# Low parts of 42 weight units formed in an earlier stage and read back from DRAM; six expert blocks placed before the last loop

## The chip, the core and the metric

The kernel runs on one core of a Trainium2 chip. A core has four engines that compute: TensorE (PE, matrix products into PSUM), VectorE (DVE), ScalarE (ACT) and GpSimd (POOL), and SyncE (SP), which here issues DMAs. Each runs its own queue of instructions in order and waits on semaphores for the others. 16 DMA engines move data between DRAM and the on-chip SBUF. A DMA is issued by an engine's queue: SP's, ACT's and POOL's are used. The metric is the time of one execution on the device, in microseconds (us).

## The reference

Two transformer blocks over one sequence of 512 tokens of width 1024, all in float32. The first has four mixers (short convolution, sparse attention, latent attention, short convolution), each with a residual. The second has neighbourhood attention with a gated MLP beside it, then a PEER layer and a last norm; its vectors `c` and `c_ctx` are multiplied with `ada_w` into scales and shifts. The parts that the change touches are the second short convolution and the PEER layer:

```python
def short_conv_mixer(xn, w_in, conv_w, conv_b, w_out):
    bg, cg, hv, z = jnp.split(xn @ w_in, 4, axis=-1)
    u = cg * hv
    y = causal_depthwise_conv_of_width_3(u, conv_w) + conv_b
    return (bg * y * jax.nn.silu(z)) @ w_out

def block(xb):                                   # PEER, per block of tokens
    q = (xb @ wq).reshape(PEER_BLOCK, PEER_HEADS, 2, PEER_HALF)
    s = jnp.einsum('thpd,hpkd->thpk', q, sub_keys)
    s_top, i_top = lax.top_k(s, PEER_TOPK)
    ...                                          # all pairs of the two halves' best
    best_s, best_pos = lax.top_k(cand_s, PEER_TOPK)
    experts = jnp.take_along_axis(cand_i, best_pos, axis=-1)
    g = jax.nn.softmax(best_s, axis=-1)
    act = jax.nn.gelu(jnp.einsum('thkd,td->thk', expert_u[experts], xb))
    return jnp.einsum('thk,thkd->td', g * act, expert_v[experts])
```

There are 16384 experts (128 x 128), 8 heads and 16 experts per head and token.

## The kernel before

**Weights.** Each float32 product is made of three TensorE passes: a weight tile of 128 x 1024 (a unit, 0.5 MB) is split into a high part `whi`, a rounded copy made by ScalarE (line 69), and a low part `wlo`, the difference, made by VectorE (line 71). `gemm_t` (lines 254 to 262) multiplies high by high, high by low and low by high: 24 matmuls a unit. `Stream` feeds the units of all layers in one list: SP loads `wraw` up to four units ahead (line 57), the split runs up to two units ahead. `wraw` has two buffers (in the PEER layer every third unit has one from a further pool), `whi` and `wlo` four each.

**The second convolution** has 32 units of `a_in` and 8 of `a_out`, each against 512 tokens. After each of the first 32 the function `side(u)` is called for work that fills the other engines: it loads a tile of `ada_w` into `adaw` (two buffers, line 861) and VectorE reduces it (line 870).

**PEER layer.** First 16 projections (`p_wq`, 24 matmuls of 512 columns each), with the top 16 found by VectorE. The steps of `choose` then form the pairs and select the experts of one block of 128 tokens. The experts are computed densely for the first 320 tokens: `gates` scatters the chosen weights into a matrix of tokens by 16384 experts. It has 80 groups of 4 tokens. For each group `marks` builds two 0/1-like operands in `w` tiles, by VectorE (lines 1306 and 1307) or, for two groups in eight, by VectorE and ScalarE (lines 1298, 1301, 1302); four TensorE matmuls (line 1329) form the matrix, ScalarE copies it out (`stage`, line 1330), and after each eighth group a 2 MB store to `gsp` in DRAM goes through ScalarE's DMA queue (line 1336).

`s_part` (lines 1153 to 1163) is a block: the scores of 128 experts from one unit of `p_u`, 24 matmuls of 320 columns, then gelu on ScalarE (line 1160). The results of the first 12 blocks stay in SBUF. Those of the next 21 go into a tile `gr` (two buffers, which the loop's reads of `gsp` use as well) and are stored to `sgd` through ScalarE's queue (line 1162). Some blocks are set between the steps of `choose`, most among the gates (line 1333), and the rest after the last gate, before the loop.

**The loop** takes the 128 units of `p_v`, multiplies block results with `gsp`, read four units at a time into `gr`, and sums. Beside it GpSimd gathers the expert rows of the remaining tokens (line 1376) and VectorE multiplies them.

**What sets the order.** The order on each engine's queue is set when the program is built: a scheduler places the instructions of the loops above on each engine by its own estimate of when they can run. So a place in the source is not a place on a queue.

Of the kernel before, what the change touches and what calls it, by code (L numbers as in the profile page):

```python
# [10 lines left out]
F32 = mybir.dt.float32  # L11
F32R = mybir.dt.float32r
# [3 lines left out]
OP = mybir.AluOpType  # L16
# [3 lines left out]
D = 1024  # L20
KD = 8
# [4 lines left out]
AHEAD = 12  # L26
MORE = 21
EARLY = 2
LAG = 2
LOOK = 2  # L30
CLOCK = (1.0, 2.3, 1.0)
TD = 3
ND = 320
# [2 lines left out]
S_AT = (1, 4, 7)  # L36
# [3 lines left out]
class Stream:  # L40
# [3 lines left out]
    def __init__(self, nc, pools, units, ahead_load, ahead_split):  # L44
        self.nc, (self.raw, self.hi, self.lo) = nc, pools
        self.more = None
        self.units, self.pos, self.loaded, self.split = units, 0, 0, 0
        self.al, self.asp = ahead_load, ahead_split
        self.r, self.hl = {}, {}
# [13 lines left out]
    def _split(self, upto):  # L63
        nc = self.nc
        while self.split < min(self.loaded, upto):
            t = self.r.pop(self.split)
            n = t.shape[1]
            h = self.hi.tile([128, n], F32R, name="whi")
            nc.scalar.activation(h, t, AF.Copy)  # L69
            l = self.lo.tile([128, n], F32R, name="wlo")  # L70
            nc.vector.tensor_tensor(l, t, h.bitcast(F32), OP.subtract)  # L71
            self.hl[self.split] = (h, l)
            self.split += 1

# [8 lines left out]
def program(ctx, tc, A, out, upto=99, dbg=None):  # L83
    nc = tc.nc
# [20 lines left out]
    dram = ctx.enter_context(tc.tile_pool(name="dram", bufs=1, space=bass.MemoryType.DRAM))  # L105

    def big(shape, dt, name):
        return bigp.tile(shape, dt, name=name, tag="big")

    def bank(shape=(128, S), pool="a"):  # L110
        return psp[pool].tile(list(shape), F32, name="bank" + pool, tag="bank" + pool)
# [60 lines left out]
    W = Stream(nc, (wraw, whi, wlo), units, 4, 2)  # L172
# [99 lines left out]
    def split(src, h, l, scale=None):  # L272
        SC.activation(h, src, AF.Copy)  # L273
        V.tensor_tensor(l, src, h.bitcast(F32), OP.subtract)  # L274
# [854 lines left out]
    def peer(nrm, lp):  # L1129
# [14 lines left out]
        sg = {}  # L1144
# [83 lines left out]
        for m in range(16):  # L1228
# [10 lines left out]
            for t in range(NT):  # L1239
                v, n = val[:, t, m // 2, m % 2], ix[:, t, m // 2, m % 2]  # L1240
# [21 lines left out]
        def columns(g):  # L1262

            nf = tmp([128, 2, 128])
            ni = tmp([128, 2, 128], I32)
            V.tensor_scalar(ni[:, 0], ei, 7, 127, OP.logical_shift_right, OP.bitwise_and)
            V.tensor_scalar(ni[:, 1], ei, 127, None, OP.bitwise_and)
            V.tensor_copy(nf, ni)
            p = bank([128, 3, 128])
            for a, x in enumerate((nf[:, 1], g, nf[:, 0])):  # L1270
                PE.transpose(p[:, a], x, ident)
            T = hn.rearrange("p (a c x) -> p a c x", a=2, c=4)[:, next(turn)]
            SC.activation(T[:, :3], p, AF.Copy)
            SC.activation(T[:, 3], p[:, 1], AF.Copy, scale=-1.0)
            cols.append(T)
# [4 lines left out]
        def halves(g):  # L1280

            V.tensor_scalar(idx, ei, 16383, None, OP.bitwise_and)
            for dst, src in ((idx_h, idx), (gate_h, g)):
                V.tensor_copy(dst[HALF:], src[HALF:, HALF:])
                SC.dma_start(dst[:HALF], src[HALF:, :HALF])
# [3 lines left out]
        def marks(n):  # L1289


            T, t0 = cols[n // 32], n % 32 * 4
            oj, oi = tmp([128, 4, 128]), tmp([128, 4, 128])

            def each(c):
                return T[:, c, t0:t0 + 4, None].to_broadcast([128, 4, 128])
            if n % 8 in BY_ACT:
                V.tensor_tensor(oj, many, each(0), OP.is_equal)
                for a in range(4):
                    w, i, nw = (T[:, c, t0 + a:t0 + a + 1] for c in (1, 2, 3))  # L1300
                    SC.activation(oi[:, a], iota, AF.Abs, scale=-1.0, bias=i)
                    SC.activation(oi[:, a], oi[:, a], AF.Relu, scale=nw, bias=w)
            else:
                for a in range(4):
                    j, w = (T[:, c, t0 + a:t0 + a + 1] for c in range(2))
                    V.tensor_scalar(oj[:, a], iota, j, w, OP.is_equal, OP.mult)
                V.tensor_tensor(oi, many, each(2), OP.is_equal)
            return oj, oi

        def gates():  # L1310

            ready, steps = [], []
            for n in range(ND // 4):
                t, r = n // 32, n % 8
                if n % 32 == 0:
                    steps = []
                    if t < TD - 1:
                        g, steps = choose(t + 1)
                        steps.append(lambda g=g: columns(g))
                        if t == TD - 2:  # L1320
                            steps.append(lambda g=g: halves(g))
                if r == 0:
                    st = big([128, 128, 32], F32, "stage")
                while len(ready) + n < min(n + 1 + LOOK, ND // 4):
                    ready.append(marks(len(ready) + n))
                oj, oi = ready.pop(0)
                ps = bank([128, 4, 128])
                for a in range(4):
                    PE.matmul(ps[:, a], oj[:, a], oi[:, a], start=True, stop=True)
                SC.activation(st[:, :, r * 4:r * 4 + 4], ps.rearrange("p t i -> p i t"), AF.Copy)  # L1330
                if steps and r:
                    steps.pop(0)()
                if len(sg) < AHEAD + MORE - 3 and r in S_AT:
                    s_part()
                if r == 7:
                    SC.dma_start(gsp[:, :, n // 8].rearrange("c p x -> p c x"), st.rearrange("p (c i) t -> p c (i t)", i=4))
            assert not steps
# [15 lines left out]
        _, steps = choose(TD)  # L1353
# [93 lines left out]
        step, used, held, fetched = 0, 0, [], []  # L1447
        clock = np.cumsum([CLOCK[(i >= MORE) + (i >= 128 - AHEAD)] for i in range(128)])
        for i in range(128):
# [40 lines left out]
        for a in range(TD):  # L1490
            for x in held:
                value_part(a, *x)
            final(a)

    def conv_layer(j):

        def layer(nrm, after, lp, src, dst):
            def side(u):
                if u == 2:
                    ada_part.cb = conditions(2 - j)  # L1500
                elif u == 3 and j == 0:
                    angles()
                elif u >= 4 and 28 * j + u - 4 < min(28 + 28 * j, 48):
                    ada_part(lp, 28 * j + u - 4)
                if u == 32 and j:
                    hc.append(ctx_norm())
            short_conv(j, nrm, after, lp, src, dst, side)
        return layer
# [146 lines left out]
```

## Time and profile before

| what | us |
|---|---|
| runs | 2806.35, 2812.2, 2813.47 |
| median of the runs | 2812.2 |
| the profiled execution | 2807.74 |
| its span (first to last instruction) | 2805.9 |
| TensorE busy (matmul) | 2658.9 (95%) |
| TensorE busy (weight load, beside the matmuls) | 2299.7 (82%) |
| VectorE busy | 2222.7 (79%) |
| ScalarE busy | 1268.8 (45%) |
| GpSimd busy | 524.2 (19%) |
| DMA moved | 586.64 MB, 209 GB/s in the mean |

The span is what the trace covers; the profiled execution's own time is 1.8 us longer. Busy shares are means over stages of very different kinds, so the rows below go stage by stage: busy time by window, which wait ended idle time, single instructions in time, and DMAs from issue to landing. The chain of waits starts at the last instruction and follows back what released each step.

### The profile page before, as it was taken

The page shows a single profiled execution, that of the slowest core. Times are in us where ns is not written, and L with a number is a line of the kernel's source. Part 1 is how long each engine was busy: PE and PEld are TensorE (multiplying, and loading weights), DVE is VectorE, ACT ScalarE, POOL GpSimd, SP SyncE. Part 2 cuts the span into 40 slices and gives each one's busy share as a digit, 9 for nine tenths or more (in the row PEclk, how much of TensorE's full clock was granted, in tenths as well). Part 3 has the DMA queues.
Part 4 walks back from the last instruction along what each step waited for, and adds up shares of the span by engine and source line. Part 5 has one row for each costly group of instructions (what it writes and reads, how often), then busy time and mean ns, then how long its engine had stood idle before and what let it go on. Part 6 is the DMA issues. An engine that isn't in the chain of part 4 may idle for free. (4 is left out here: it accounts for less than half of the span.)

```text
span 2805.9 us, 40937 instructions
## 1 busy us (share of the span) xinstructions
PE 2658.9 (95%) x14563; PEld 2299.7 (82%) x14563; DVE 2222.7 (79%) x5367; ACT 1268.8 (45%) x2284; POOL 524.2 (19%) x388
## 2 busy tenths in 40 slices
PE   8999999999999999999999897878999999999987
PEld 7888889987887888888887787877789888889875
DVE  8966987763897756565435899896999899999998
ACT  4234346653886223444422335574444344344443
POOL 0000000000000000000000000003465676666661
PEclk9999999999999999999999999998999999999999
DMA  6653321133114624332345224569999999999996
GB/s 217 211 169 117 102 76 54 57 122 108 54 53 164 227 98 133 127 101 73 98 151 166 77 97 136 182 185 323 388 410 409 376 409 409 409 406 408 409 408 245
DMA packets 217037, 586.64 MB, mean 209 GB/s; under 512 B 20736, under 2 KB 74240, under 8 KB 216704
## 3 DMA queue, kind: packets, MB, share of 16 engines
q1 hardware_dynamic: 116080, 356.13, 36.3%
q0 software_dynamic: 55296, 201.35, 18.1%
q10 hardware_dynamic: 45456, 26.54, 3.2%
q8 instruction: 115, 1.88, 0.3%
q14 instruction: 90, 0.74, 0.1%
HBM read 538.53 MB, written 45.38 MB: 208 GB/s over the span
## 5 line engine op out<-in xcount | busy, mean ns | idle before, releaser
L69 ACT ACTIVATE whi<-wraw 128x1024 fp32r<-128x1024 f32 x491 | 515.5, 1051 | 924.4 <-PE bankg L261 341.3
L71 DVE TENSOR_TENSOR wlo<-wraw,whi 128x1024 fp32r<-128x1024 f32 x491 | 593.2, 1209 | 209.9 <-ACT whi L69 209.0
L1376 POOL DMA_INDIRECT it<-in_p_urows_dram,idx_h x64 | 83.6, 1306 | 1988.7 <-ACT stage L1330 1905.1
L260 PE MATMUL bankg<-XH,whi 128*128 128x512 f32 x1032 | 405.9, 394 | 13.7 <-ACT whi L69 8.7
L261 PE MATMUL bankg<-XL,whi 128*128 128x512 f32 x1032 | 404.7, 392 | 0.0
L262 PE MATMUL bankg<-XH,wlo 128*128 128x512 f32 x1032 | 404.5, 392 | 0.0
L262 PE MATMUL banka<-XH,wlo 128*128 128x320 f32 x1024 | 318.4, 311 | 6.6 <-DVE wlo L71 6.6
L260 PE MATMUL banka<-XH,whi 128*128 128x320 f32 x1024 | 320.2, 313 | 1.8 <-ACT w L1258 1.5
L261 PE MATMUL banka<-XL,whi 128*128 128x320 f32 x1024 | 317.5, 310 | 0.0
L1383 DVE CUSTOM_DVE_ANT_0 it<-it,hn 128x1024 f32<-128x1024 f32 x192 | 230.5, 1217 | 14.3 <-DMA it<-in_p_urows_dram,idx 14.3
L260 PEld LDWEIGHTS bankg<-XH,whi 128*128 128x128 f32 x1032 | 195.0, 189 | 54.8 <-ACT whi L69 11.1
L262 PEld LDWEIGHTS bankg<-XH,wlo 128*128 128x128 f32 x1032 | 194.7, 189 | 40.7 <-DVE wlo L71 0.8
L261 PEld LDWEIGHTS bankg<-XL,whi 128*128 128x128 f32 x1032 | 194.9, 189 | 39.3 <-DVE XL L237 0.3
L1376 POOL DMA_INDIRECT it<-in_p_urows_dram,idx x128 | 186.7, 1459 | 88.9 <-DVE act L1383 59.8
L262 PEld LDWEIGHTS banka<-XH,wlo 128*128 128x128 f32 x1024 | 193.3, 189 | 8.8 <-DVE wlo L71 8.7
L260 PEld LDWEIGHTS banka<-XH,whi 128*128 128x128 f32 x1024 | 193.6, 189 | 7.3 <-ACT w L1258 1.7
L261 PEld LDWEIGHTS banka<-XL,whi 128*128 128x128 f32 x1024 | 193.5, 189 | 3.8
L1376 POOL DMA_INDIRECT it<-in_p_v_dram,idx x128 | 170.8, 1335 | 103.0 <-DVE ysum L1393 90.9
L1403 PE MATMUL bankg<-whi,wx 128*128 128x512 f32 x384 | 155.4, 405 | 17.8 <-ACT wx L273 17.6
L420 PE MATMUL bankg<-whi,XH 128*128 128x256 f32 x576 | 166.0, 289 | 6.0 <-DVE OL L661 1.5
L422 PE MATMUL bankg<-whi,XL 128*128 128x256 f32 x576 | 164.1, 286 | 0.0
L1406 PE MATMUL bankg<-whi,wx 128*128 128x512 f32 x384 | 155.3, 406 | 8.7 <-DVE wx L274 8.5
(555 smaller groups left out, 6053.8 us busy)
## 6 DMA issues: line engine op xcount, KB each, us to landing
wraw<-in_p_u_dram SPq DMA_DIRECT2D x128, 512.0 KB, 6.8
wraw<-in_p_v_dram SPq DMA_DIRECT2D x128, 512.0 KB, 7.2
wraw<-in_a_in_dram SPq DMA_DIRECT2D x64, 512.0 KB, 3.8
adaw<-in_ada_w_dram SPq DMA_DIRECT2D x48, 512.0 KB, 4.5
gsp<-stage ACTq DMA_DIRECT2D x10, 2048.0 KB, 11.2
gr<-gsp SPq DMA_DIRECT2D x32, 640.0 KB, 8.3
wraw<-in_b_in_dram SPq DMA_DIRECT2D x24, 512.0 KB, 3.6
wraw<-in_a_out_dram SPq DMA_DIRECT2D x16, 512.0 KB, 3.3
```

The lines of the kernel that those rows point to most:

```text
L69: nc.scalar.activation(h, t, AF.Copy)
L71: nc.vector.tensor_tensor(l, t, h.bitcast(F32), OP.subtract)
L260: PE.matmul(ps, a, xh[:, k, :], start=k == 0, stop=False)
L261: PE.matmul(ps, a, xl[:, k, :], start=False, stop=False)
L262: PE.matmul(ps, b, xh[:, k, :], start=False, stop=k == kk - 1)
L420: PE.matmul(ps, a, wh, start=k == 0, stop=False)
L422: PE.matmul(ps, b, wh, start=False, stop=k == len(blocks) - 1)
L1376: G.indirect_dma_start(out=u, out_offset=None, in_=rows, in_offset=bass.IndirectOffsetOnAxis(ap=(idx_h if two else idx)[:, n:n + 1], axis=0))
L1383: V.tensor_tensor_reduce(u, u, hn, 1.0, 0.0, OP.mult, OP.add, a)
L1403: PE.matmul(po[a][b], parts[0], w[0][:, ds], start=i == 0, stop=False)
L1406: PE.matmul(po[a][b], parts[1], w[0][:, ds], start=False, stop=i == 127)
```

## The change

Three edits. A new function `low_parts` runs in the second convolution's `side(u)`. For the first 42 units of the PEER layer (16 `p_wq` and 26 `p_u`) it loads the unit through SP (`preraw`, four buffers), one call later splits it on ScalarE and VectorE (`prehi`, `prelo`), and one call later still stores the low part to `lod` in DRAM through SP; one unit a call for 22 calls, two a call after that. `Stream._split` then loads the low part of such a unit from `lod` through GpSimd's queue in place of the subtraction; the high part is still made from `wraw` by ScalarE. And among the gates blocks are set until six are left (three before) for the place before the loop.

```diff
--- before.py
+++ after.py
@@ -28,6 +28,7 @@
 EARLY = 2
 LAG = 2
 LOOK = 2
+PRE = 42
 CLOCK = (1.0, 2.3, 1.0)
 TD = 3
 ND = 320
@@ -44,6 +45,7 @@
     def __init__(self, nc, pools, units, ahead_load, ahead_split):
         self.nc, (self.raw, self.hi, self.lo) = nc, pools
         self.more = None
+        self.low = {}
         self.units, self.pos, self.loaded, self.split = units, 0, 0, 0
         self.al, self.asp = ahead_load, ahead_split
         self.r, self.hl = {}, {}
@@ -65,10 +67,14 @@
         while self.split < min(self.loaded, upto):
             t = self.r.pop(self.split)
             n = t.shape[1]
+            key = self.units[self.split][0]
             h = self.hi.tile([128, n], F32R, name="whi")
             nc.scalar.activation(h, t, AF.Copy)
             l = self.lo.tile([128, n], F32R, name="wlo")
-            nc.vector.tensor_tensor(l, t, h.bitcast(F32), OP.subtract)
+            if key in self.low:
+                nc.gpsimd.dma_start(l, self.low[key])
+            else:
+                nc.vector.tensor_tensor(l, t, h.bitcast(F32), OP.subtract)
             self.hl[self.split] = (h, l)
             self.split += 1
 
@@ -1330,7 +1336,7 @@
                 SC.activation(st[:, :, r * 4:r * 4 + 4], ps.rearrange("p t i -> p i t"), AF.Copy)
                 if steps and r:
                     steps.pop(0)()
-                if len(sg) < AHEAD + MORE - 3 and r in S_AT:
+                if len(sg) < AHEAD + MORE - 6 and r in S_AT:
                     s_part()
                 if r == 7:
                     SC.dma_start(gsp[:, :, n // 8].rearrange("c p x -> p c x"), st.rearrange("p (c i) t -> p c (i t)", i=4))
@@ -1492,10 +1498,40 @@
                 value_part(a, *x)
             final(a)
 
+
+    lod = dram.tile([PRE, 128, D], F32, name="lod")
+    early = [("p_wq", m) for m in range(16)] + [("p_u", i) for i in range(PRE - 16)]
+
+    def low_parts(lp, todo, raw, low, n):
+
+        for k, l in low:
+            nc.sync.dma_start(lod[k], l.bitcast(F32))
+            W.low[early[k]] = lod[k]
+        low.clear()
+        for k, t in raw:
+            h = lp.tile([128, D], F32R, name="prehi", bufs=2)
+            l = lp.tile([128, D], F32R, name="prelo", bufs=4)
+            split(t, h, l)
+            low.append((k, l))
+        raw.clear()
+        for _ in range(n):
+            if todo:
+                k = todo.pop(0)
+                name, i = early[k]
+                t = lp.tile([128, D], F32, name="preraw", bufs=4)
+                nc.sync.dma_start(t, A[name][i])
+                raw.append((k, t))
+
     def conv_layer(j):
 
         def layer(nrm, after, lp, src, dst):
+            todo, raw, low = list(range(PRE)) if j else [], [], []
+
             def side(u):
+                low_parts(lp, todo, raw, low, 1 if u < 22 else 2)
+                if u == 4 * KD:
+                    low_parts(lp, todo, raw, low, 0)
+                    assert not (todo or raw or low)
                 if u == 2:
                     ada_part.cb = conditions(2 - j)
                 elif u == 3 and j == 0:
```

**SP in the second convolution.** The rows go from `a_in` unit to `a_in` unit; `adaw` are the tiles of `ada_w`. Before:

```order
197 L57 DMA wraw<-in_a_in_dram 128x1024 x2
198 L861 DMA adaw<-in_ada_w_dram 128x1024 x2
199 L57 DMA wraw<-in_a_in_dram 128x1024
200 L861 DMA adaw<-in_ada_w_dram 128x1024 x2
201 L57 DMA wraw<-in_a_in_dram 128x1024
202 L861 DMA adaw<-in_ada_w_dram 128x1024 x2
203 L57 DMA wraw<-in_a_in_dram 128x1024
204 L861 DMA adaw<-in_ada_w_dram 128x1024 x2
205 L57 DMA wraw<-in_a_in_dram 128x1024
206 L887 DMA ctx<-in_ctxT_dram 128x2048
207 L57 DMA wraw<-in_a_in_dram 128x1024 x20
```

After, about the middle of the stage, on the same queue:

```order
230 L59 DMA wraw<-in_a_in_dram 128x1024
231 L1508 DMA lod<-prelo 128x1024
232 L1522 DMA preraw<-in_p_wq_dram 128x1024
233 L59 DMA wraw<-in_a_in_dram 128x1024
234 L867 DMA adaw<-in_ada_w_dram 128x1024
235 L1508 DMA lod<-prelo 128x1024
236 L1522 DMA preraw<-in_p_wq_dram 128x1024
237 L59 DMA wraw<-in_a_in_dram 128x1024
238 L867 DMA adaw<-in_ada_w_dram 128x1024
```

and towards its end:

```order
274 L59 DMA wraw<-in_a_in_dram 128x1024
275 L1508 DMA lod<-prelo 128x1024 x2
276 L1522 DMA preraw<-in_p_u_dram 128x1024 x2
277 L59 DMA wraw<-in_a_in_dram 128x1024
278 L1508 DMA lod<-prelo 128x1024 x2
279 L1522 DMA preraw<-in_p_u_dram 128x1024 x2
280 L59 DMA wraw<-in_a_in_dram 128x1024
```

Where two `adaw` stood between two `wraw`, there is now one, with a store of `lod` and a load of `preraw`; the `adaw` loads reach further into the stage, and where they have ended two loads and two stores stand between two `wraw`. Before, the last 20 `a_in` units followed each other with nothing between.

**VectorE where the first gates' marks begin** (lines 1306 and 1307 before, 1312 and 1313 after), with the last steps of `choose` ahead of them (`rk`, `cand`, `best`). Before:

```order
2637 L1197 MAX_INDEX rk<-cand_14777,best_14783 128x8 x7
2638 L1194 MAX best_14783<-cand_14778 128x8
2639 L1195 MATCH_REPLACE cand_14778<-best_14783,cand_14778 128x56
2640 L1197 MAX_INDEX rk<-cand_14777,best_14783 128x8 x6
2641 L71 TENSOR_TENSOR wlo<-wraw,whi 128x1024
2642 L1306 TENSOR_SCALAR w_16341<-iota,hn 128x128 x4
2643 L1307 TENSOR_TENSOR w_16342<-iota,hn 128x512
```

After:

```order
2644 L1193 TENSOR_TENSOR cand_15072<-vi 128x8x2 x3
2645 L1195 TENSOR_TENSOR cand_15072<-vi 128x8x8
2646 L1207 TENSOR_TENSOR g<-best_15078 128x128
2647 L1198 MAX best_15078<-cand_15072 128x8 x8
2648 L1312 TENSOR_SCALAR w_16636<-iota,hn 128x128 x4
2649 L1313 TENSOR_TENSOR w_16637<-iota,hn 128x512
```

The subtraction that stood ahead of the first marks is gone. On GpSimd's queue 42 loads of `wlo` from `lod` now stand ahead of the first gather (`it`), where the queue had no work.

**ScalarE after the last gate's copy** (`stage`), up to the loop's first multiplied tiles (`wx`). Before:

```order
1397 L1330 ACTIVATE stage<-banka 128x128x4 x4
1398 L1336 DMA gsp<-stage 128x32x128
1399 L1160 ACT_TABLE_LOAD
1400 L1160 ACTIVATE gr<-banka 128x320 x2
1401 L1162 DMA sgd<-gr 128x320 x2
1402 L69 ACTIVATE whi<-wraw 128x1024 x2
1403 L1160 ACTIVATE gr<-banka 128x320
1404 L1368 ACTIVATE hn<-banka 128x512
1405 L1162 DMA sgd<-gr 128x320
```

After:

```order
1430 L1166 ACTIVATE gr<-banka 128x320 x2
1431 L1168 DMA sgd<-gr 128x320 x2
1432 L72 ACTIVATE whi<-wraw 128x1024 x2
1433 L1166 ACTIVATE gr<-banka 128x320
1434 L72 ACTIVATE whi<-wraw 128x1024
1435 L1168 DMA sgd<-gr 128x320
1436 L1166 ACTIVATE gr<-banka 128x320
1437 L1168 DMA sgd<-gr 128x320
1438 L72 ACTIVATE whi<-wraw 128x1024
1439 L1166 ACTIVATE gr<-banka 128x320
1440 L1168 DMA sgd<-gr 128x320
```

The `gsp` store, the table load and the first two results stand as before; where one more block result and its store followed, there are now four.

## Rows read from the trace of the kernel before

**Rows 1.** Busy us by stretch (x instructions): PE, PEld, DVE, ACT, POOL; clock, DMA share, GB/s.
```profile
880.00:1090.00 210.00, 208.10 (x924) 172.01 (x923) 133.78 (x189) 66.23 (x82) 0.00 (x0) 1.00 0.52 174
...
880.00:920.00 40.00, 38.10 (x172) 31.32 (x171) 32.02 (x52) 17.66 (x24) 0.00 (x0) 1.00 0.92 312
...
1552.00:1662.00 110.00, 108.35 (x535) 90.88 (x536) 102.63 (x580) 41.59 (x58) 0.00 (x0) 0.98 0.25 78
1662.00:1724.00 62.00, 48.00 (x326) 46.99 (x325) 61.28 (x427) 27.93 (x50) 0.00 (x0) 0.92 0.39 134
1724.00:1772.00 48.00, 38.62 (x270) 37.77 (x269) 47.49 (x287) 27.13 (x59) 0.00 (x0) 0.90 0.49 149
1772.00:1820.00 48.00, 44.16 (x324) 43.65 (x323) 36.60 (x104) 33.08 (x76) 0.00 (x0) 0.96 0.60 189
1820.00:1869.00 49.00, 38.20 (x272) 37.09 (x270) 48.69 (x271) 30.74 (x64) 0.00 (x0) 0.93 0.56 171
1869.00:1905.00 36.00, 27.90 (x197) 25.23 (x198) 34.96 (x99) 31.52 (x77) 0.00 (x0) 0.95 0.77 221
...
1960.00:2700.00 740.00, 721.86 (x3859) 634.68 (x3859) 707.34 (x959) 305.01 (x495) 468.74 (x339) 1.00 1.02 404
```

**Rows 2.** TensorE in time, two matmuls 24 apart: start us, duration us.
```profile
1536.00 0.39 PE L260 MATMUL bankg<-MH,whi 128*128 128x512 f32 x1
...
1541.44 0.39 PE L260 MATMUL bankg<-MH,whi 128*128 128x512 f32 x1
```

**Rows 3.** TensorE's waits, 1662 to 1905: us in total, times, longest us.
```profile
PE banka L1329 <- DVE w L1307: 25.3, 7, 10.2
PE banka L1329 <- ACT w L1302: 12.8, 10, 4.6
```

**Rows 4.** VectorE's subtractions by line; 1540 to 1659, 1659 to 1905, 1772 to 1820.
```profile
L71 DVE TENSOR_TENSOR wlo<-wraw,whi 128x1024 fp32r<-128x1024 f32 x15 | 18.1, 1214 | 7.4 <-ACT whi L69 7.4
...
L71 DVE TENSOR_TENSOR wlo<-wraw,whi 128x1024 fp32r<-128x1024 f32 x32 | 38.6, 1213 | 6.9 <-ACT whi L69 6.8
...
L71 DVE TENSOR_TENSOR wlo<-wraw,whi 128x1024 fp32r<-128x1024 f32 x7 | 8.5, 1221 | 6.8 <-ACT whi L69 6.8
```

**Rows 5.** Chain that ended last, 1540 to 1960: start us, us, engine, tile, line.
```profile
1904.87 0.15 PE banka L260
...
1908.39 0.15 PE banka L260
...
1922.04 4.37 DMA gr<-gsp
```

**Rows 6.** ScalarE in time, 1904 to 1930 (ACTq: DMA issues): start us, us, last wait.
```profile
1906.03 0.37 ACTq L1336 DMA_DIRECT2D gsp<-stage  x1
...
1912.01 4.00 ACTq L1162 DMA_DIRECT2D sgd<-gr  x2
...
1921.53 0.44 ACT L1160 ACTIVATE gr<-banka 128x320 f32<-128x320 f32 x1 [3.46 <-DMA sgd<-gr]
```

**Rows 7.** Splits by line, 880 to 1090: busy us, mean ns | idle us before, releasers.
```profile
L71 DVE TENSOR_TENSOR wlo<-wraw,whi 128x1024 fp32r<-128x1024 f32 x40 | 48.8, 1222 | 7.2 <-ACT whi L69 7.2
...
L69 ACT ACTIVATE whi<-wraw 128x1024 fp32r<-128x1024 f32 x38 | 40.2, 1060 | 114.5 <-issue 63.5 <-PE bankg L261 39.7 <-DMA wraw<-in_a_in_dram 7.7
```

**Rows 8.** DMAs: count, KB each, median us to landing; last from the whole run.
```profile
gsp<-stage ACTq DMA_DIRECT2D x1, 2048.0 KB, 15.0
...
sgd<-gr ACTq DMA_DIRECT2D x18, 160.0 KB, 1.8
...
wraw<-in_p_u_dram SPq DMA_DIRECT2D x128, 512.0 KB, 6.8
```

**Rows 9.** GpSimd and VectorE in time, then VectorE's line 1183 (ns min/median/max).
```profile
1927.06 0.95 POOL L1376 DMA_INDIRECT it<-in_p_urows_dram,idx_h  x1 [0.30 <-DVE w L1456]
...
1927.94 0.22 DVE L1183 TENSOR_SCALAR w<-w 128x128 f32<-128x128 f32 x1
...
L1183 DVE TENSOR_SCALAR w<-w x5: 175/216/220, 1627.0 to 1927.9; 128x128 f32<-128x128 f32 x3, 128x64 f32<-128x64 f32 x2
```

## The prediction

> **What bounds the kernel now.** I read the busy time by stretch first [rows 1], because the share over the whole span mixes stages with different limits. Four stages matter here.
>
> The second convolution (880 to 1090 us) is TensorE's: 208.1 of 210 us busy at full clock, VectorE at 133.8, ScalarE at 66.2, the DMA rings at 174 GB/s [rows 1]. A unit there is 24 matmuls, and two of them 24 places apart start at 1536.00 and 1541.44 [rows 2], so I count 5.44 us a unit. The query projections of the last layer (1552 to 1662) are TensorE's too, 108.4 of 110.
>
> From 1662 to 1904.87, where the gates are done and the first kept block starts [rows 5], the picture turns. VectorE is busy 61.3 of 62, 47.5 of 48, 48.7 of 49 and 35.0 of 36 us, and only between 1772 and 1820 has it room (36.6 of 48) [rows 1]. The waits say the same: TensorE stood 25.3 us for VectorE's `w` (the gate matrices' marks), and 12.8 us for ScalarE's [rows 3]. So a VectorE instruction taken out of that stretch is worth its own time, except in the window with room, as long as TensorE or ScalarE does not become late instead.
>
> The expert loop (1960 to 2700) runs with the rings at 404 GB/s, a share of 1.02 [rows 1]: it is bound by bytes, the change leaves its bytes alone, and I let it keep its length and only shift.
>
> **Part 1: the subtractions leave.** VectorE makes 15 of them in 1540 to 1659 and 32 from there to 1905, at 1.21 us each [rows 4], 47 in all. The changed kernel makes 42 fewer, so 5 stay. The 15 lie where TensorE bounds: worth nothing. Of the 27 others 7 lie in the window with room [rows 4]: nothing. The remaining 20 lie where VectorE is full: 20 x 1.21 = 24.2 us. TensorE can follow, since its waits for VectorE (25.3) are more than that; ScalarE's 12.8 stay [rows 3]. I take 24.2; the low end is 10, if ScalarE catches more than half of what VectorE gives back, the high end 25.3, all that TensorE waits for there.
>
> **Part 2: the low parts come back by DMA.** 42 loads of 0.524 MB (128 x 1024 x 4 bytes) on GpSimd's queue, whose engine has nothing before 1905 (0.00 us in every window up to there [rows 1]). Such an issue has no row; the nearest is an indirect load of the same size, 0.95 us [rows 9], so 42 x 0.95 = 40 us of an idle engine. The new wait: each load waits for the buffer that TensorE frees four units earlier, and behind it in GpSimd's queue stand only the loads of later units. A load is asked for two units ahead of its use, so it has at least 2 x 3.52 = 7.0 us (1904.87 to 1908.39 is one block [rows 5]) when blocks follow each other, and more with gates between them or in the projections. A load of an expert unit lands 6.8 us after its issue in the median [rows 8]. So it is hidden: cost 0 to 5 us, taken as 0. The stretches ran at 78 to 221 GB/s [rows 1], which leaves room for the bytes.
>
> A row bears on this load's price from the other side. One VectorE TENSOR_SCALAR ran 0.22 us from 1927.94, beside GpSimd's 0.95 us issue that began at 1927.06, against a median of 0.216 for its line [rows 9]: not held up, but a single case with 0.07 us in common. The Trainium skill, SBUF — State Buffer, section "Who interferes with whom", says that GpSimd and a VectorE `tensor_scalar` in a two-port mode shut each other out for a whole instruction, whoever comes first; by it the change would put GpSimd's issues right among the marks. The one row does not show it, and it is rival (c).
>
> **Part 3: the low parts are formed in the second convolution.** Added: 42 loads and 42 stores of 0.524 MB on SP's queue, 42 copies on ScalarE (1.06 us) and 42 subtractions on VectorE (1.22) [rows 7]. ScalarE goes from 66 to 111 of 210 us, VectorE from 134 to 185: both fit on average. The queue is the question. In the order shown with the change each unit first has four transfers (`wraw`, `adaw`, `preraw`, `lod`), 2.10 MB, and then for some ten units five (two `preraw`, two `lod`), 2.62 MB. At the loop's 404 GB/s these take 5.19 and 6.49 us against TensorE's 5.44: only the ten units are over, by 1.05 us each, 10.5 us, and the splits run two units (10.9 us) ahead of TensorE. That lead was full: ScalarE waited 39.7 us for TensorE to free a `whi` and 7.7 us for a `wraw` [rows 7]. Cost 0. At the rate that this stage's own busiest 40 us give, 312 GB/s at a share of 0.92 [rows 1], 339 when full, the two kinds take 6.19 and 7.73 us: 23 x 0.75 + 10 x 2.29 = 40 us over, less the lead 29. New waits stand in the same places: on SP a `lod` store waits for a subtraction, and behind it the `wraw` that TensorE needs; on VectorE a subtraction waits for a `preraw` that may land late, and behind it `wlo` and the emptying of PSUM. Nothing that TensorE waited for there goes away, so no gain. The bytes per share rise with load (174 at 0.52, 312 at 0.92, 404 at 1.02 [rows 1]), so I stand nearer the loop's rate and take 5 us, range 0 to 29.
>
> **Part 4: six blocks for the loop's eve.** Between the last gate and the loop TensorE waits for the last `gsp` store to land (issued 1906.03, 15.0 us [rows 6, 8]) and for `gr` to be read back (from 1922.04 [rows 5]). Three more blocks, 10.6 us, fit in the hole. At the gates their leaving is no gain, since VectorE and not TensorE was late there, and they lengthen the eve: their results go through the two `gr` buffers and ScalarE's queue. Count from the last gate. Now: the stores of the first two results wait in ScalarE's queue behind the `gsp` store until +11.1 (1912.01 plus 4.00), the third result waits for one of them to land, +16.7 (1921.53) [rows 6], and the first `gr` load starts at +17.2. Then: the first two as now; results three and four at +16.7 and +18.5 with a `whi` copy between; the third's store lands 1.8 us [rows 8] after its issue, so five goes at +20.6, its store lands at +23.1, and only then is a buffer free for the first `gr` load: 5.9 us later than now. Range 3 (stores come off earlier) to 12 (each as late as the first).
>
> **Sum**: -24.2 + 0 + 5 + 5.9 = -13.3 us. Against the profiled execution's 2807.74 that is 2794.4. It lies 1.4 over the fastest run shown and 4.5 under the median of 2812.2, which less 13.3 is 2798.9. I say 2797, between.
>
> **Rivals.** (a) Slower: the second convolution's feed breaks. The queue keeps its 339 GB/s and TensorE stands 29 us there. For it: a queue asked for 385 to 480 GB/s, one unit's wraw behind four other transfers, two `wraw` buffers. Against it: the waits of 39.7 against 7.7 before. It decides from 18.3 us, what parts 1 and 4 leave; with 29: 2807.7 - 18.3 + 29 = 2818, or 2823 from the median. I say 2822. Chance 0.21.
> (b) No change: ScalarE takes over at the gates. It is held behind each `gsp` store by the next `sgd` store (the 4.00 us of rows 6), and TensorE waits 12.8 us for its marks already. Part 1 gives 10: 2807.7 - 10 + 5 + 5.9 = 2809, against the median 2813. Chance 0.12.
> (c) GpSimd's issues stop VectorE: the 22 or so loads that lie beside the gates (27 less 5) cost it 0.95 us each, 21 us back: 2794.4 + 21 = 2815. Chance 0.06. The Trainium skill's page SBUF — State Buffer is its source.
> (d) That the change doesn't do what it says: the order has 42 loads on GpSimd in the place of 42 subtractions, so this is out.
>
> **How the numbers follow.** Forecast 0.61, its own range 2785 to 2808: part 1 between 16 and 25, part 4 between 3 and 10, part 3 up to 10. 0.3% is 8.4 us, about what a measurement of this kernel can tell from no change: faster is below 2803.8, slower above 2820.6. Of the forecast 0.50 is faster and 0.11 the same. Of (a) 0.17 is slower and 0.04, shorter stalls, the same; (b) and (c), 0.18, are mostly the same, with 0.02 for slower. Together: faster 0.50, same 0.31, slower 0.19. The range reaches from 2783 (profiled run less 25.3 and little given back) to 2823, part-way into (a), leaving out the rest of (a) and the best tail.
>
> **What would show it.** Right: no line 71 work for the first 42 units after 1540; TensorE's 25.3 us of waits for `w` down to some 5; the last gate some 24 us nearer to the first projection; the first `gr` load some 23 us behind the last gate; the second convolution longer by less than 10 us. Wrong: TensorE idle between 900 and 1130 with `wlo` or `whi` as releaser (a); growing waits for ScalarE's `w` (b); longer TENSOR_SCALAR marks (c); a loop that changes its length.

## The result, and the profile after

The changed kernel takes 2827.4 us in the median of 6 runs (2820.9 to 2830.2), the kernel before 2811.5 beside it: a ratio of 1.0056, 95% interval 1.0042 to 1.0070. It is slower by 16 us, where 14 faster was forecast. The profiled execution took 2825.25, its span 2823.1 (before 2807.74 and 2805.9), so the two profiles differ by 17.2.

Where the 17.2 us lie is read off a few instructions that both kernels have in the same number. The first pair of rows is TensorE's line of the third pass (count: ns min/median/max, first and last start). `OH` is what the units of a convolution's second half (`a_out`) are multiplied with, and the start of its last matmul is taken as the end of the second convolution; the last `XH` with 512 columns ends the projections. Before:

```profile
L262 PE MATMUL bankg<-XH,wlo x608: 387/389/628, 913.8 to 1658.7; 128*128 128x512 f32 x152
...
L262 PE MATMUL bankg<-OH,wlo x120: 387/389/476, 866.8 to 1133.8; 128*128 128x512 f32 x120
```

After (its lines stand six further down):

```profile
L268 PE MATMUL bankg<-XH,wlo x608: 387/389/632, 914.8 to 1690.4; 128*128 128x512 f32 x152
...
L268 PE MATMUL bankg<-OH,wlo x120: 387/389/632, 866.9 to 1168.3; 128*128 128x512 f32 x120
```

The gates' matmuls (line 1335, 1329 before), the first `gr` load and the loop's first matmul were read in the same way:

| us | before | after | difference |
|---|---|---|---|
| end of the second convolution | 1133.8 | 1168.3 | +34.5 |
| from there to the end of the projections | 524.9 | 522.1 | -2.8 |
| selection steps, to the first gate | 53.9 | 44.0 | -9.9 |
| gates | 192.0 | 174.9 | -17.1 |
| last gate to the loop's first matmul | 22.9 | 37.0 | +14.1 |
| loop, to the span's end | 878.4 | 876.8 | -1.6 |

The eve is the stretch from the last gate to the loop's first matmul. So the gain was there (27.0 us in steps and gates), and the second convolution and the eve gave back 48.6. By stretch the convolution looks thus (columns as in rows 1; "the rings" below are the 16 DMA engines, their share is the next to last column). First the end of the stage before, then three stretches after:

```profile
1090.00:1130.00 40.00, 39.55 (x177) 32.26 (x176) 27.88 (x55) 17.60 (x31) 0.00 (x0) 1.00 0.52 172
```

```profile
880.00:1090.00 210.00, 205.80 (x904) 169.35 (x903) 162.38 (x213) 97.27 (x111) 0.00 (x0) 0.99 0.91 325
1090.00:1130.00 40.00, 21.49 (x95) 17.48 (x93) 24.79 (x40) 16.91 (x23) 0.00 (x0) 0.79 0.89 339
...
1980.00:2720.00 740.00, 725.65 (x3887) 638.47 (x3886) 710.46 (x958) 304.44 (x496) 467.17 (x339) 1.00 1.02 405
```

Up to 1090 TensorE lost little (205.8 us busy against 208.1 [rows 1]), with the rings at a share of 0.91 in place of 0.52. Then, from 1090 to 1130, it stood for nearly half of the 40 us, of which 39.55 were busy before. The loop is as it was [rows 1]. TensorE's waits from 870 to 1140 name the place (us in total, times, longest):

```profile
PE banka L249 <- DVE ctx L235: 15.3, 1, 15.3
PE bankg L266 <- DVE X L334: 8.2, 1, 8.2
PE banka L256 <- DVE rs_yn L206: 3.2, 1, 3.2
```

The first is the norm of `ctx`, the second block's context. SP's queue in time tells why it was late:

```profile
1105.81 8.90 SPq L1508 DMA_DIRECT2D lod<-prelo  x4
1114.77 0.46 SPq L893 DMA_DIRECT2D ctx<-in_ctxT_dram  x1
1115.32 0.76 SPq L59 DMA_DIRECT2D wraw<-in_a_out_dram  x1
```

The `ctx` load left at 1114.77, behind the last four stores of low parts; before, it left at 956.79:

```profile
956.79 0.33 SPq L887 DMA_DIRECT2D ctx<-in_ctxT_dram  x1
```

The next `a_out` weight unit stood behind the same stores. That the order puts `ctx` there explains one wait; whether it is the cause was tested.

### The profile page after: what moved, and what is told of

The parts are those of the page before. It is cut to its first block, busy times and chain, and to the rows that moved or that the text cites. A ratio compares the mean times of both kernels' runs of the same rounds, so it can differ in the third digit from the quotient of the medians.

```text
span 2823.1 us, 41223 instructions
## 1 busy us (share of the span) xinstructions
PE 2661.4 (94%) x14563; PEld 2298.8 (81%) x14563; DVE 2223.0 (79%) x5367; ACT 1310.8 (46%) x2326; POOL 542.8 (19%) x430
## 5 line engine op out<-in xcount | busy, mean ns | idle before, releaser
L77 DVE TENSOR_TENSOR wlo<-wraw,whi 128x1024 fp32r<-128x1024 f32 x449 | 542.9, 1210 | 189.5 <-ACT whi L72 184.1
L75 POOL DMA_DIRECT2D wlo<-lod x42 | 22.7, 540 | 1791.0 <-DMA wraw<-in_p_wq_dram 1558.7
L1399 DVE SCALAR_TENSOR_TENSOR ysum<-it,act,ysum 128x1024 f32<-128x1024 f32 x127 | 162.5, 1280 | 3.7 <-DMA it<-in_p_v_dram,idx 2.8
```

Source lines behind the costliest of these rows:

```text
L75: nc.gpsimd.dma_start(l, self.low[key])
L1399: V.scalar_tensor_tensor(y, u, a, y, OP.mult, OP.add)
```

## Experiments

All numbers of a stage below are read as in the table. The kernel before ran beside each group, at 2810.8 to 2812.2 in the median. The unchanged convolution ended at 1133.5 to 1135.0 in three profiles.

**Is it the order on SP's queue?** `ctx` asked for early, at `side(12)` (`ctx_load` is the load taken out of `ctx_norm`):

```diff
...
+                if u == 12 and j:
+                    early_ctx.append(ctx_load())
...
-                    hc.append(ctx_norm())
+                    hc.append(ctx_norm(early_ctx[0]))
```

> One edit to the changed kernel: the 1 MB load of ctx is asked for in the 12th call of side and not in the 32nd; it then stands six steps earlier on SP's queue, ahead of the last 12 stores of low parts, and all else is as in the changed kernel. Theory A (the ctx load, held behind the last stores on SP, is what TensorE waits for): TensorE's waits of 15.3 us for ctx and 3.2 us for rs_yn go, and most of the 8.2 us for X; some 20 us less than the changed kernel's 2827, so 2803 to 2809. Theory B (everything on SP's queue behind the last four stores is late, the a_out weight units too, issued at 1115.3): TensorE then waits for wlo or whi instead; 5 to 10 us less, 2817 to 2822. Theory C (the rings are full, 390 GB/s, and no order helps): no change, 2824 to 2830.

Measured: 2818.4, ratio 1.0019 (1.0007 to 1.0031), 9 us less than the changed kernel. The convolution ends at 1158.1. TensorE's waits from 870 to 1175:

```profile
PE bankg L266 <- DVE X L334: 8.0, 2, 7.1
PE bankg L268 <- DVE wlo L77: 7.3, 4, 4.7
PE bankg L266 <- DVE w L319: 3.1, 3, 1.8
```

The wait for `ctx` is gone, and others took its place: the weights of `a_out` themselves are late. Theory A falls; B fits so far (2817 to 2822 was expected of it).

The stores on GpSimd's queue, so that nothing on SP's stands behind them:

```diff
-            nc.sync.dma_start(lod[k], l.bitcast(F32))
+            nc.gpsimd.dma_start(lod[k], l.bitcast(F32))
```

> One edit to the changed kernel: the 42 stores of low parts go through GpSimd's queue, which is idle in that stage, and not through SP's. The same bytes are moved in the same stage; what leaves is that ctx, the weight units and the preraw loads stand behind stores that wait for VectorE. Theories A and B (SP's order): of the 34.5 us that the second convolution lost 25 or more come back, 2797 to 2803, under the kernel before. Theory C (full rings): the loss stays above 20 us, 2815 to 2827.

Measured: 2817.9, ratio 1.0025 (1.0012 to 1.0039); the convolution ends at 1159.2. Of 34.5 us 9 came back, not 25, so B alone falls too, and theory C's range (2815 to 2827) holds. The waits now lie in the middle of the stage:

```profile
PE bankg L266 <- DVE w L319: 9.9, 2, 5.0
PE bankg L266 <- DVE ld L334: 6.5, 2, 6.2
PE bankg L266 <- DVE ada L881: 3.3, 1, 3.3
```

and the stretches of the same kernel say what they have in common, the two columns at the end:

```profile
920.00:960.00 40.00, 40.00 (x181) 33.09 (x180) 35.97 (x55) 18.31 (x22) 3.98 (x8) 0.98 1.00 385
960.00:1000.00 40.00, 37.29 (x163) 29.96 (x161) 30.29 (x40) 15.05 (x17) 3.46 (x7) 1.00 0.98 369
1000.00:1040.00 40.00, 34.36 (x134) 27.76 (x135) 34.03 (x43) 20.13 (x22) 5.84 (x11) 0.87 0.99 372
```

With the stores off SP's queue the rings run full, and TensorE waits in these same stretches. That the one causes the other is argued from the rows, not shown apart. Both edits in one kernel:

> Both edits that gave back 9 us each, in one kernel: ctx asked for early, and the stores on GpSimd's queue; 42 units are still formed. If the two order effects are separate losses, both come back: the last matmul of the convolution's second half near 1142 in place of 1168, the time 2805 to 2811. If full rings set a floor (84 transfers of 0.524 MB, with a share of 0.95 to 1.00 from 900 to 1090 once the stores stood on GpSimd's queue): it stays where each of them left it, that matmul at 1155 to 1161, the time 2815 to 2820.

Measured: 2820.6, ratio 1.0031 (1.0020 to 1.0042); the convolution ends at 1160.2, with shares of 0.93 to 1.00 from 880 to 1090. The two 9 us are the same 9 us. Some 25 us are left in each of the three orders. With the stores on GpSimd's queue the rings stood at 0.97 from 880 to 1090 and at 0.32 from 1090 to 1130, so room was left at the end; an order that spreads the transfers into it was not tried.

**Transfers or engine work?** First all of the forming taken out; the loads of `wlo` read the inputs:

```diff
-            todo, raw, low = list(range(PRE)) if j else [], [], []
+            todo, raw, low = [], [], []
+            if j:
+                for name, i in early:
+                    W.low[name, i] = A[name][i]
```

> The changed kernel without the forming: no preraw load, no split and no store in the second convolution; the 42 loads of wlo on GpSimd's queue read the unit itself from the inputs, the same size and place in time, so those weights are wrong and the output too. What it leaves is part 1, 2 and 4 of the prediction. From the trace of the changed kernel: the selection steps and gates 27 us shorter, the eve 14 us longer, the second convolution as before: 2811 - 27 + 14 = 2798, 2793 to 2803. If instead the loads from DRAM slow the projections or the gates by what they bring, or the 34.5 us are not the forming's, it stays at 2811 or above.

Measured: 2795.4, ratio 0.9941 (0.9919 to 0.9964). The convolution ends at 1133.5, steps and gates are 24.5 us shorter than before, the eve 14.6 longer. So the 34.5 us are the forming's, and parts 1 and 2 of the prediction did what they were to do. Then the transfers without the splits:

```diff
-            h = lp.tile([128, D], F32R, name="prehi", bufs=2)
-            l = lp.tile([128, D], F32R, name="prelo", bufs=4)
-            split(t, h, l)
-            low.append((k, l))
+            low.append((k, t))
...
-                t = lp.tile([128, D], F32, name="preraw", bufs=4)
+                t = lp.tile([128, D], F32, name="preraw", bufs=8)
```

> The changed kernel with the transfers of the forming alone: 42 loads of preraw and 42 stores to lod in the same calls on the same queue, but no copy and no subtraction between them (the unit itself is stored, so the low parts are wrong and the output too; preraw has eight buffers). Beside it stands the kernel without forming at 2795.4. Theory C (the rings: 80.5 MB in a stage that gives 339 to 385 GB/s, and what TensorE needs queues among it): 15 to 30 us over 2795, so 2810 to 2825, with TensorE waiting for weights. Theory D (the transfers fit, and it is the splits, held in order on ScalarE and VectorE by late preraw loads, that hold what TensorE waits for): 2795 to 2803.

Measured: 2818.3, ratio 1.0027 (1.0016 to 1.0038); the convolution ends at 1158.5, and TensorE waits again at the last step, with no split of the forming ahead of it:

```profile
PE banka L249 <- DVE ctx L235: 11.3, 1, 11.3
PE bankg L266 <- DVE X L334: 9.0, 2, 8.1
PE banka L256 <- DVE rs_yn L206: 3.2, 1, 3.2
```

And the splits without the transfers, from one tile:

> The other half: 42 copies and 42 subtractions in the same calls, from one preraw tile that is loaded once, with no other load and no store (the 42 loads of wlo read the inputs, so the output is wrong). Theory C: the engines have room (ScalarE 111, VectorE 185 of 210 us), 2795 to 2800. Theory D in its form that late loads are needed for the loss: the same. If the engines' work itself delays TensorE: 2805 or more.

Measured: 2798.2, ratio 0.9952 (0.9935 to 0.9968), 2.8 us over the kernel without forming; its convolution ends 7 to 9 us later in the profile (1142.2), so the engines' work is not quite free. Theory D falls, and theory C's times hold: the transfers alone cost 23 of the 32 us that the forming costs (2818.3 and 2827.4 against 2795.4), the splits alone 2.8, and some 6 come only with both. What C had named, waits for weights, was not what the transfers alone showed: TensorE waited for `ctx`, which again left behind four stores. So that run does not tell full rings from SP's order. The kernel with both edits speaks for the rings, since nothing on SP's queue stands behind a store there and it loses as much; but its `preraw` loads still stand among the weights on that queue, so it is no proof. Loads and stores were not told apart.

**How much fits?** Low parts of the 26 `p_u` units alone, one a call, `ctx` early, three blocks for the eve:

```diff
-PRE = 42
+PRE = 26
...
-    early = [("p_wq", m) for m in range(16)] + [("p_u", i) for i in range(PRE - 16)]
+    early = [("p_u", i) for i in range(PRE)]
...
-                low_parts(lp, todo, raw, low, 1 if u < 22 else 2)
+                low_parts(lp, todo, raw, low, int(u >= 5))
...
-                if len(sg) < AHEAD + MORE - 6 and r in S_AT:
+                if len(sg) < AHEAD + MORE - 3 and r in S_AT:
```

> A version: low parts of the 26 p_u units alone (the 16 of the projections, which TensorE bounds, stay VectorE's), one a call from the sixth call of side, so 52 transfers in place of 84 and never five between two weight units; ctx asked for early; three blocks kept for the eve. If the rings' load sets the loss: it falls from 34 to 5 to 12 us, the selection steps and gates keep their 27 us less the 5 that the blocks add, the eve is as before: 2811 - 27 + 5 + 9 = 2798, 2790 to 2802, under both kernels. If the loss comes from any forming beside the convolution: 2808 or more.

Measured: 2784.4, ratio 0.9904 (0.9886 to 0.9923): 26 us faster than before, 43 faster than the changed kernel, and better than expected. The convolution ends at 1133.6, with no loss, steps and gates are 17.8 us shorter, the projections 3, the eve is 22.9 as before. In 880 to 1130 it moved this (packets, MB, mean rate; then queue q1, SP's: packets, MB, share of the 16 rings):

```profile
DMA packets 21381, 70.54 MB, mean 282 GB/s; under 512 B 2383, under 2 KB 2639, under 8 KB 21238
...
q1 hardware_dynamic: 21366, 70.34, 80.2%
```

against the changed kernel's:

```profile
DMA packets 23610, 81.71 MB, mean 327 GB/s; under 512 B 2624, under 2 KB 2880, under 8 KB 23468
...
q1 hardware_dynamic: 23596, 81.53, 90.4%
```

The same with `ctx` where the changed kernel asks for it:

> The 26-unit version with ctx asked for where the changed kernel has it (in the last call of side, behind most stores). If the number of transfers is what matters (52 in place of 84) and ctx was late only because the stores ahead of it were: the convolution keeps its 0 to 3 us of loss, the time 2783 to 2789. If ctx behind the stores costs by itself: 10 to 20 us more, 2794 or above.

Measured: 2787.5, ratio 0.9908 (0.9891 to 0.9924). Its profile, of the slowest of its four runs, shows 6.6 us of loss in the convolution (0 to 3 were expected); the medians differ by 3.1. With fewer transfers the late `ctx` costs little. Then 30 units (`PRE = 30`, from the second call on):

> The 26-unit version with 30 units, still one a call, from the second call of side on: 60 transfers, 4.2 MB more in the same stage, and 4 subtractions fewer of the 8 that VectorE still makes among the gates. The 26-unit version moved 70.5 MB in 880 to 1130 at a share of 0.81 and lost nothing there; the changed kernel 81.7 MB and lost 34.5 us. If the loss begins only near the full share, 75 MB are still free and the four subtractions give up to 4.8 us: 2779 to 2786. If 70.5 MB was already the edge: 2789 or more, with TensorE's waits in the stage above 6 us.

Measured: 2797.9, ratio 0.9939 (0.9919 to 0.9960). That is 13.5 us over the 26 units. In the profile 7.1 of them lie in the convolution, which ends at 1140.7, 2.5 in the projections and 2.8 in the gates. It moved 73.26 MB in the same 250 us:

```profile
DMA packets 21917, 73.26 MB, mean 293 GB/s; under 512 B 2432, under 2 KB 2688, under 8 KB 21774
...
q1 hardware_dynamic: 21902, 73.07, 84.1%
```

The four subtractions fewer gave nothing either: the gates took 186.9 us against 184.1. Its waits from 1640 to 1920 show both engines late in turn:

```profile
PE banka L1338 <- DVE w L1316: 14.7, 6, 5.3
PE banka L1338 <- ACT w L1311: 13.9, 9, 4.1
```

Side by side, the share of the rings from 880 to 1130 (the column of the stretches, all queues together) and the convolution's loss in the profile: 0.81 and nothing (26 units), 0.80 and 6.6 us (the same, `ctx` late), 0.84 and 7 us (30 units), 0.86 to 0.91 and 24 to 34 us (42 units, in every order and with the transfers alone). The share was not varied by itself: the number of splits, the calls they come in and the place of `ctx` change with it, and each loss is that of one profile. So more transfers cost more; where the step lies, and why, stays open.

**The eve.** The changed kernel with three blocks kept (`AHEAD + MORE - 3`):

> One edit to the changed kernel: three blocks are kept for the eve, as before, and three more lie among the gates. If the eve's length (31.8 us from the last gate to the first gr load, against 17.4 before) is set by the kept blocks' results that pass through the two gr buffers, it goes back to 17 to 19 us, and the gates grow by 0 to 10.6 us, for VectorE now has room in them: 2813 to 2824. If the eve waits for something else (the gsp store, the weights' subtractions), no change or slower: 2826 to 2835.

Measured: 2815.8, ratio 1.0016 (1.0002 to 1.0029), 11.6 us less than the changed kernel. From the last gate to the first `gr` load 17.0 us in place of 31.8; the gates take 179.8 in place of 174.9. And the kernel before with six:

```diff
-                if len(sg) < AHEAD + MORE - 3 and r in S_AT:
+                if len(sg) < AHEAD + MORE - 6 and r in S_AT:
```

> The kernel before with one edit: six blocks kept for the eve in place of three. From the pair of the changed kernel and its version with three (11.5 us): the eve, 22.9 us from the last gate to the loop's first matmul, grows to 36 to 38, the gates get 0 to 5 us shorter: 9 to 14 us slower than before, 2820 to 2825. If the eve's growth needs the changed loads (GpSimd's queue, contention): less than 4 us, 2815 or below.

Measured: 2820.6, ratio 1.0026 (1.0015 to 1.0037), 8.9 us slower. The eve is 37.3 us, the gates 188.8 (192.0 before). The three blocks cost nearly as much without the other edits. What holds them is in ScalarE's rows of the changed kernel:

```profile
1916.72 6.01 ACTq L1168 DMA_DIRECT2D sgd<-gr  x2
...
1926.12 0.33 ACTq L1168 DMA_DIRECT2D sgd<-gr  x1
1926.93 0.43 ACT L1166 ACTIVATE gr<-banka 128x320 f32<-128x320 f32 x1
...
1932.29 0.44 ACT L1166 ACTIVATE gr<-banka 128x320 f32<-128x320 f32 x1 [2.69 <-DMA sgd<-gr]
```

The fifth result (1932.29) waits until the third's store, issued at 1926.12, has landed, and the first `gr` load until the fifth's has. The chain that ended last, 1900 to 1950, runs through both stores (start us, us):

```profile
1926.12 6.09 DMA sgd<-gr
...
1932.76 8.35 DMA sgd<-gr
1941.12 4.06 DMA gr<-gsp
```

Results in tiles of the temporaries in place of the two `gr` buffers:

```diff
-            sg[i] = gr_tile()[:, :ND] if wait else sg_tile(i)
+            sg[i] = tmp([128, ND]) if wait else sg_tile(i)
```

> One edit to the changed kernel: the results of blocks 12 to 32 go into tiles of the pool of temporaries (eight buffers) and not into the two gr buffers that the loop's reads use. If the eve is long because results and the first gr loads pass through two buffers in turn, each held until its store lands: from the last gate to the first gr load 31.8 us fall to 17 to 22, and the time by 10 to 14 to 2813 to 2817. If the stores on ScalarE's queue or the blocks themselves set it: less than 4 us, 2823 or more.

Measured: 2822.7, ratio 1.0040 (1.0024 to 1.0055). The first `gr` load comes 15.8 us after the last gate, sooner than the 17 to 22 expected, but the time falls by 4.7 only, where 10 to 14 were expected. The results now share buffers with the marks, and the gates take 184.4. And the loop does not start with `gr`: its first matmul comes 33.0 us after the last gate, behind `whi` copies of the loop's units, which wait for loads:

```profile
1941.79 1.06 ACT L72 ACTIVATE whi<-wraw 128x1024 fp32r<-128x1024 f32 x1 [7.55 <-DMA wraw<-in_p_v_dram]
...
1948.82 0.47 ACT L279 ACTIVATE wx<-w 128x320 fp32r<-128x320 f32 x1 [0.43 <-DVE w L1188]
```

So the two buffers hold the `gr` load, and with that taken away ScalarE's copies, which wait for the loop's weights, hold the loop. The test shows the first and not that it is all.

## Why the prediction was wrong

**Part 1 came out in size.** Forecast -24.2 us. With three blocks kept (so that part 4 is not in it) steps and gates are 22.2 us shorter than before (43.9 and 179.8 against 53.9 and 192.0). The 15 subtractions in the projections were worth nothing, as forecast: that stretch is 2.8 us shorter in the changed kernel, but also 3.0 in the 26-unit version, which keeps them, and 2.2 in the kernel before with six blocks, which keeps all. The sign that was named for it failed: TensorE's waits for `w` did not fall to 5. In the changed kernel, 1690 to 1945:

```profile
PE banka L1335 <- DVE w L1313: 21.8, 14, 4.8
...
PE banka L1335 <- ACT w L1308: 4.6, 6, 1.3
```

With three blocks kept they are 14.1 for VectorE and 12.2 for ScalarE. VectorE still ends last at the gates [rows 3], its waits are only shorter: the longest was 10.2 us, ahead of the first gate, and is 4.8. That it was full in a window did not mean that it would be empty afterwards. And not all of the 22.2 us are waits. By TensorE's rows over steps and gates (before, and with three blocks kept), its idle time fell from 47.3 to 30.6 us, and the same 1396 matmuls took 193.1 us in place of 198.6. The clock granted was 1.00 in the steps and 0.97 in the gates, 0.95 and 0.92 before. These 5.5 us were not in the prediction's account, so its 24.2 is near for reasons that it named only in part.

**Part 2 was right**, and rival (c) did not come. GpSimd's 42 issues and VectorE's marks in the changed kernel (ns min/median/max):

```profile
L75 POOL DMA_DIRECT2D wlo<-lod x42: 530/530/727, 1559.2 to 1813.6; - x42
```

```profile
L1312 DVE TENSOR_SCALAR w<-iota,hn x240: 299/342/381, 1732.6 to 1906.9; 128x128 f32<-128x128 f32 x120
```

The same marks before:

```profile
L1306 DVE TENSOR_SCALAR w<-iota,hn x240: 325/340/352, 1710.8 to 1902.2; 128x128 f32<-128x128 f32 x120
```

An issue costs 0.53 us, not the 0.95 of the indirect load [rows 9], and the marks' median is 342 ns after 340, their longest 381: with 240 of them no microsecond is lost. But the test was weaker than the prediction had it: only 12 of the 42 issues came after the first mark, not 22, and only two of them, at 1742.02 and 1779.14, while marks ran. The groups of four marks there took 1.11 and 1.10 us, as such groups do elsewhere in the gates (1.09 to 1.12). The Trainium skill, SBUF — State Buffer, section "Who interferes with whom", says that GpSimd and a VectorE instruction in a two-port mode shut each other out for a whole instruction. An estimate by it for a mark held up behind an issue is the sum of 0.34 and 0.53, near 0.9 us. No mark shows that here, and no row tells which mode the marks ran in. No wait of TensorE for a loaded `wlo` is among its waits.

**Part 3 failed.** It was put at 5 us, range 0 to 29; it is 34.5 in the profile, 32 in the medians. The step that failed is its sum: a unit's bytes at a mean rate against TensorE's 5.44 us, less a lead of two units. Two things in it were wrong.

First the test by the mean. The stage moved 81.71 MB in 250 us at 327 GB/s, below the 339 that I had as the other end. That end's 29 us came near by luck: by its sum the last ten `a_in` units lose most, and there, from 1040 to 1090, TensorE was busy 49.78 of 50 us. Nor was it only the rate. Where the rings stood full they gave 367 to 392 GB/s (the stores on GpSimd's queue, 920 to 1040; the changed kernel, 1040 to 1090). At 385 the same sum gives some 3 us, and the kernel that ran at 385, 369 and 372 lost 25.

Second, the lead and who stands behind. The splits' lead, which I took off the sum, was gone. ScalarE stood for the loads of the forming itself, with the `whi` copies behind in its queue, and hardly waited for TensorE any more (870 to 1140):

```profile
ACT prehi L279 <- DMA preraw<-in_p_u_dram: 36.2, 18, 5.7
ACT prehi L279 <- DMA preraw<-in_p_wq_dram: 32.1, 14, 4.8
...
ACT whi L72 <- PE bankg L267: 8.7, 6, 2.6
```

Before, that last wait came to 55.4 us in the same window (39.7 from 880 to 1090 [rows 7]). I had named late `preraw` loads for VectorE alone. They are not the whole cause, since the transfers without these copies lost 25 us too. As those who would be late I named `wraw`, `wlo` and PSUM. SP's queue did not show its debt where it arose: TensorE lost 5 us up to the last `a_in` unit, while the forming fell behind, and the rest at the end, where the last stores stood ahead of `ctx` and of the `a_out` units, which I did not follow to SP's end. Moving `ctx` or the stores only moved the waits (9 of 34.5 us).

Once TensorE had stood there, its clock fell too: granted 0.50, the lower of its two levels of 1.2 and 2.4 GHz, after it had been idle from 1110 on, and full again from 1150 (us, busy columns as above). An estimate of its cost is 2 us: 37 matmuls in 1140 to 1150, 46 of the same kind in the next 10 us.

```profile
1110.00:1120.00 10.00, 0.03 (x1) 0.00 (x0) 3.00 (x4) 2.11 (x2) 0.00 (x0) 0.68 0.85 313
1120.00:1130.00 10.00, 1.46 (x6) 1.22 (x6) 6.91 (x20) 4.72 (x11) 0.00 (x0) 0.50 0.69 242
...
1140.00:1150.00 10.00, 10.00 (x37) 8.05 (x36) 4.60 (x6) 2.69 (x4) 0.00 (x0) 0.79 0.58 180
1150.00:1160.00 10.00, 10.00 (x46) 8.29 (x45) 4.53 (x6) 3.29 (x4) 0.00 (x0) 1.00 0.65 189
```

**Part 4 had the mechanism and missed the size.** The chain through the two `gr` buffers is what the rows show. Its price was put at 5.9 (3 to 12); the first `gr` load came 14.4 us later. The term that failed is the store, which I let land in 1.8 us [rows 8], twice in the chain. It took 6.1 and 8.4 us. The 1.8 is the median of the 18 stores issued up to 1900, among the gates. The trace of the kernel before had the eve's own three (1900 to 1930), and one of them on its chain, right ahead of the `gr` load [rows 5]:

```profile
sgd<-gr ACTq DMA_DIRECT2D x3, 160.0 KB, 6.3
```

```profile
1915.50 6.34 DMA sgd<-gr
```

With 6.3 for each of the two the sum would have been 5.9 + 9.0 = 14.9 us. Why a store takes longer there was not tested; it runs beside the loop's first weight loads and gathers. The blocks' leaving was worth 3 to 5 us at the gates, not nothing. Net +9 to +12, the two measured differences.

**Rival (a)** was the one that came, at 0.21: TensorE stands in the second convolution, time 2822 against 2827 measured. Its number is near, its place was another than its sign said: `ctx` and not `wlo` or `whi` was the releaser, and the 29 us in it are those of the sum above. The loop kept its length, as forecast.

## What to carry to other kernels

Before work is moved into a stage that "has room", take the bytes that it adds and the share that the rings would then have in that stage, not the mean of its engines: here 26 units at 0.81 were free and 30 at 0.84 were not. Follow an in-order queue to its end, and name what stands behind the last of the added transfers, since here the debt was paid there. Price a transfer by rows of the stretch in which it will run: the same store took 1.8 us among the gates and 6.3 on the eve. And move only what pays: 16 of the 42 units served a stage that TensorE bounds; without them, with `ctx` early and three blocks kept, the same idea is 26 us faster than the kernel before.

## What was not expected of the hardware

A plain DMA issue on GpSimd's queue took 0.53 us, little over half of the indirect one. With 84 further transfers of 0.5 MB the rings gave 325 GB/s at a share of 0.91 from 880 to 1090 with the stores on SP's queue, 368 at 0.97 when the stores left it, and the stage was 9 us shorter, no more.
